# A different order of work at two places of a gated MLP: the first channel block, and the head of the first pair

## The chip, the cores and the metric

The kernel runs on one core of a Trainium2 chip. The metric is device time in microseconds (us) of one execution. The engines are TensorE (PE; its weight loads are listed apart as PEld), VectorE (DVE), ScalarE (ACT), GpSimd (POOL) and SyncE (SP, which issues the weight loads from memory).

## The reference

Two layers over 256 tokens of width 2048, in float32. Layer 0 mixes tokens by grouped-query attention, layer 1 by dilated sliding-window attention; each is followed by the gated MLP that this case is about, and a last RMS norm ends it. Cut to the MLP:

```python
D_MODEL, SEQ, D_FF, DEPTH = 2048, 256, 5632, 2

def conv_ffn(h, w_up, conv_w, conv_b, w_down):
    u = h @ w_up                                  # 256 x 2048 times 2048 x 11264
    u = depthwise_conv_width_3(u, conv_w) + conv_b   # over token positions
    gate, val = jnp.split(u, 2, axis=-1)
    return (jax.nn.silu(gate) * val) @ w_down     # 256 x 5632 times 5632 x 2048

for i in range(DEPTH):
    h = h + mixer(rms_norm(h, mix_norm[i]))
    h = h + conv_ffn(rms_norm(h, ffn_norm[i]), w_up[i], conv_w[i], conv_b[i], w_down[i])
return rms_norm(h, final_norm)
```

## The kernel before

**Products.** A float32 product is made of three passes. Every operand is split into a high part (typed F32R) and a low part, the rest; the kernel sums high x high, high x low and low x high into one accumulator. Weights arrive as raw tiles of 128 x 1024 numbers (512 KB), one load each on SP's queue, into six buffers. For each tile ACT copies the high part (`wh`, L126) and DVE subtracts it from the raw tile (`wl`, L127); there are three buffers for such pairs, four in the down projection. So every tile costs one ACT and one DVE operation, whatever is done with it.

**Up projection.** A column block is 512 of the 11264 columns. A gate block and a value block make a channel block; there are eleven, numbered 0 to 10, worked in two halves (0 to 5, 6 to 10). A column block takes four feeds, one for each quarter (0 to 3) of the 2048 inputs; a feed (`feed`) loads and splits two raw tiles and issues 24 matmuls: two tiles, two 128-row pieces each, two token halves, three passes. The accumulators are two PSUM banks. Normally `project` runs four feeds of the gate and then four of the value. Channel block 0 is special: the transposed input of the last input quarter is still being made then (`late_transpose`), so `project2` runs quarters 0, 1, 2 of the gate and of the value, then `drain` writes out what is pending, then quarter 3 of each.

**Post-processing.** When a column block is done, a generator (`up_post`) follows: ACT evacuates the two banks and DVE transposes them in 32 x 32 blocks; sixteen small copies, shared by POOL, DVE and ACT, place them in order (L430, L432, L434); ACT and DVE do the convolution; for a gate, Silu, for a value, the product with the gate and the split into high and low halves, or, in a block that the down projection treats with seven products, the seven combinations it needs (`glu_forms`). The taps of the convolution come from `taps`, called once behind gate block 0: three transposes of `cr` (L399), loaded at the start of the MLP. Generators wait in the list `pending`. `step`, called twice in a feed and once in a unit of a pair, moves the first one on by one stage; during the up projection it moves the first two.

**Down projection.** A half of the channel blocks is multiplied into `h` for two column blocks n0 and n1 at a time, a pair (`project_pair`). Its accumulators are all eight banks: C11, C21 (the two token halves for n0), C12, C22 (for n1), M1, M5, M6, M7. Its work is a list of units. A usual unit ("c", channel block, 0 to 3) takes one raw tile and 12 matmuls for two of the C banks; four of them make a channel block. A seven-product unit ("P", channel block, product) takes one tile and six matmuls; seven of them, in the order 1, 2, 5, 3, 7, 6, 4, make a channel block in the manner of Strassen and Winograd. Products 5, 7, 6 and 4 need a sum of two weight blocks first, a DVE operation of its own (L228). Product 2 adds to C11, 3 to C12, 4 to C21. Seven-product channel blocks are the first and third of a first half, and the first of a second half: 16 usual and 14 seven-product units in a first half, 16 and 7 in a second. The unit list takes one usual unit, then a seven-product and a usual one by turns, then the usual ones that are left. Before the first unit of the last channel block `drain` completes what is pending, in the first pair.

After the last seven-product unit `combine` starts (L601 to L613: the M banks are added into `h`), and after C21's last unit `first_half` adds C11 and C21 into `h` (L374, `add_residual`). C12 and C22 are added at the end. A first half has two pairs, columns (0, 1) and (2, 3), one behind the other on the same banks; a second half has one pair, and `project` for the other two column blocks.

**What sets the order.** The kernel writes its instructions in the order above, and a planner places them on the engines by its own timing: on each engine the ready instruction that was written first goes first, and the two split operations and the sums of weight blocks count as written 45 instructions earlier (`AHEAD`). An operation that is ready early can so run ahead of its place in the text; once placed, an engine's order is fixed.

Of the kernel before, what the change touches and what calls it, by code (L numbers as in the profile page):

```python
# [18 lines left out]
NPAIR = 11  # L19
# [5 lines left out]
ORDER = (1, 2, 5, 3, 7, 6, 4)  # L25
PLACE = "pava"
AHEAD = 45
NWARM = 11


@with_exitstack
def tile_encoder(ctx: ExitStack, tc: tile.TileContext, x, xT, w_a, w_ao, q_gain, k_gain, w_b, w_bo,
# [67 lines left out]
    def drain(keep=0):  # L100
        while len(pending) > keep:
            step()
# [20 lines left out]
    def split_raw(r, release=True):  # L123
        wh, wl = new_hl()
        with tc.high_priority(offset=AHEAD):
            nc.scalar.activation(wh, r, AF.Copy)  # L126
# [47 lines left out]
    def new_acc():  # L174
        bank_at[0] = (bank_at[0] + 2) % 4
        return [bank(bank_at[0] + m, "acc") for m in range(2)]

    def project(w, n, lhs, kgs, by_m=False):
        accs = new_acc()
        for i, kg in enumerate(kgs):  # L180
            end = i == len(kgs) - 1
            feed(accs, lhs, kg, w[n, kg], i == 0, end, by_m and end)
        return accs

    def project2(w, n0, n1, lhs, kgs, late, first_done, hook=None):
        a0, a1 = new_acc(), new_acc()
        early = len(kgs) - late
        for k, part in enumerate((range(early), range(early, len(kgs)))):
            if k == 1:
                drain()  # L190
            for accs, n in ((a0, n0), (a1, n1)):
                for i in part:
                    kg = kgs[i]
                    mid = hook and hook(n == n0, kg)
                    feed(accs, lhs, kg, w[n, kg], i == 0, i == len(kgs) - 1,
                         pieces=4 if hook and i < 2 else 2, mid=mid)
                if k == 1 and n == n0:
                    first_done(a0)
        return a1

    def project_pair(w, n0, n1, lhs, forms, units, late, early_done, n0_done):
        home = {1: "M1", 2: "C11", 3: "C12", 4: "C21", 5: "M5", 6: "M6", 7: "M7"}
        place = ("M1", "M5", "M6", "M7", "C11", "C21", "C12", "C22")
        b = bank_at[0]
        acc = {k: bank((4, 5, 6, 7, 2 - b, 3 - b, b, b + 1)[i], "acc") for i, k in enumerate(place)}

        def touched(u):
            return (home[u[2]],) if u[0] == "P" else (("C11", "C21"), ("C12", "C22"))[u[2] // 2]

        first, last = {}, {}  # L210
        for i, u in enumerate(units):
            for k in touched(u):
                first.setdefault(k, i)
                last[k] = i
        blocks = {}
        sums = {5: ("11", "12"), 7: ("12", "22"), 6: ("22", "11"), 4: ("21", "22")}

        def block(kg, b):
            if (kg, b) not in blocks:
                blocks[kg, b] = load_raw(w, (n0, n1)[int(b[1]) - 1], kg, int(b[0]) - 1)  # L220
            return blocks[kg, b]

        def prepare(u):
            kind, kg, p = u
            if kind == "P" and p in sums:
                dst, src = (block(kg, b) for b in sums[p])
                with tc.high_priority(offset=AHEAD):
                    nc.vector.tensor_tensor(dst, dst, src, ALU.add)  # L228
                if p == 6:
                    done_raw(blocks.pop((kg, "11")))  # L230
                elif p == 4:
                    done_raw(blocks.pop((kg, "22")))

        last_s = max(i for i, u in enumerate(units) if u[0] == "P")
        for i, (kind, kg, p) in enumerate(units):
            if i == late:
                drain()
            if kind == "c":
                r = load_raw(w, (n0, n1)[p // 2], kg, p % 2)
            else:  # L240
                b = {1: "11", 2: "21", 3: "22", 5: "11", 7: "12", 6: "22", 4: "21"}[p]
                r = block(kg, b)
            if i + 1 < len(units):
                prepare(units[i + 1])
            wh, wl = split_raw(r, kind == "c" or p in (7, 4))
            if kind == "P" and p in (7, 4):
                blocks.pop((kg, b))
            todo = []
            if kind == "c":
                for j in range(2):  # L250
                    for m, k in enumerate(touched((kind, kg, p))):
                        todo.append((k, *at(lhs[4 * kg + 2 * (p % 2) + j], m), j))
            else:
                xh, xl = forms[kg][p]
                for j in range(2):
                    todo.append((home[p], xh[:, j * P:(j + 1) * P], xl[:, j * P:(j + 1) * P], j))
            fresh = {k for k in acc if first[k] == i}
            for k, xh, xl, j in todo:
                nc.tensor.matmul(acc[k], xh, wh[:, j, :], start=k in fresh, stop=False)  # L259
                fresh.discard(k)  # L260
                nc.tensor.matmul(acc[k], xl, wh[:, j, :], start=False, stop=False)  # L261
            todo.sort(key=lambda t: (t[0], t[3]))
            for k, xh, xl, j in todo:
                nc.tensor.matmul(acc[k], xh, wl[:, j, :], start=False, stop=last[k] == i and j == 1)  # L264
            if i == last_s:
                early_done(acc)
            if i == last["C21"]:
                n0_done(acc)
            step()
        return acc  # L270
# [111 lines left out]
    def ffn(l, hT, ss_in, g_next, last, side=None):  # L382
        with tc.tile_pool(name=nm("wpool"), bufs=1) as wp, tc.tile_pool(name=nm("fpool"), bufs=1) as fp:
# [111 lines left out]
            kgs = list(range(4))  # L495
            for hf, (p0, p1) in enumerate(HALVES):
# [8 lines left out]
                for p in range(p0, p1):  # L505
                    if p - p0 in SKG[hf]:
                        fm = forms[p - p0] = {f: new_form() for f in (1, 7, 2, 5, 4, 6, 3) + (0,) * hf}
                        if hf:
                            for kt in range(4):
                                slots[4 * (p - p0) + kt] = [  # L510
                                    tuple(t[:, kt % 2 * P:(kt % 2 + 1) * P] for t in fm[f])
                                    for f in ((1, 0), (2, 4))[kt // 2]]
                    else:
                        slots.update({4 * (p - p0) + j: new_form() for j in range(4)})
                    cg, cv = ([fp.tile([P, 2, NT], F32, tag=t, name=nm(t), bufs=3) for _ in range(2)]
                              for t in ("cg", "cv"))

                    def after(hh, cg=cg, cv=cv, slots=slots, forms=forms, kg=p - p0):
                        if kg in forms:
                            return glu_forms(cg[hh], cv[hh], forms[kg], hh)  # L520
                        return glu(cg[hh], cv[hh], slots, 4 * kg + 2 * hh)

                    if p == 0:
                        def gate_done(a, cg=cg):
                            taps()
                            start(up_post(a, 0, cg))

                        va = project2(w_up[l], p, NPAIR + p, hT, kgs, 1, gate_done)
                    else:
                        start(up_post(project(w_up[l], p, hT, kgs), p, cg))  # L530
                        va = project(w_up[l], NPAIR + p, hT, kgs)
                    start(up_post(va, NPAIR + p, cv, after))
                    if p == 1 and side is not None:
                        spare.append(side(wp, fp))
# [41 lines left out]
                np_ = p1 - p0  # L576
# [7 lines left out]
                        fin.append(f)  # L584
                cs = [("c", k, i) for k in range(np_) if k not in SKG[hf] for i in range(4)]
                ps = [("P", k, p) for k in SKG[hf] for p in ORDER]
                per = max((len(cs) - 4) // len(ps), 1)
                units = [cs.pop(0)]
                for u in ps:
                    units += [u] + [cs.pop(0) for _ in range(per)]  # L590
                units += cs
                late_at = next(i for i, u in enumerate(units) if u[1] == np_ - 1)
                hl_ring.insert(0, (wp, 9))

                def hcol(m, n):
# [27 lines left out]
                    done((a["C11"], a["C21"]), n0)  # L623

                def pair(n0, n1, late):
                    acc = project_pair(wd, n0, n1, slots, forms, units, late_at if late else None,
                                       lambda a: start(combine(a, n0, n1)),
                                       lambda a: first_half(a, n0, n1))
                    done((acc["C12"], acc["C22"]), n1)
                    finished(n0, n1)  # L630
# [395 lines left out]
    hT, ss = mixer_a()  # L1026
    hT, ss = ffn(0, hT, ss, 2, False, bias_lines)
    hT, ss = mixer_b(hT, ss)
# [85 lines left out]
```

## Time and profile before

| what | value |
|---|---|
| time, median of 3 runs | 2283.02 us (2282.5 to 2283.18) |
| the profiled execution | 2283.76 us |
| its span, first to last instruction | 2281.9 us |
| around the span | 1.86 us |
| matmuls | 10169 |
| mean granted TensorE clock | 0.999 |
| up projection, channel blocks 0 to 5, layer 0 | from 269.48 us to 539.45 |
| the two pairs of its first half | to 666.25 |
| channel blocks 6 to 10 | to 883.85 |
| the pair of the second half | to 938.66 |
| the same five edges in layer 1 | 1552.69, 1818.02, 1944.68, 2162.28, 2217.60 |

Times in the rows below are microseconds from the span's start, and nanoseconds where a row gives the mean of one instruction. A row of the instructions in order of time gives start, length, engine, line, operation, tiles, shape and count; in brackets is how long the engine was idle before it, and what it waited for last. A row of grouped instructions gives the count, then busy time and the mean of one, then the idle time before them. Matmuls overlap: they are listed as about 390 ns long and start closer together than that, so a stretch's length over its matmuls tells more than their lengths.

### The profile page before, as it was taken

The page shows a single profiled execution, that of the slowest core. Times are in us where ns is not written, and L with a number is a line of the kernel's source. Part 1 is how long each engine was busy: PE and PEld are TensorE (multiplying, and loading weights), DVE is VectorE, ACT ScalarE, POOL GpSimd, SP SyncE. Part 2 cuts the span into 40 slices and gives each one's busy share as a digit, 9 for nine tenths or more (in the row PEclk, how much of TensorE's full clock was granted, in tenths as well). Part 3 has the DMA queues.
Part 4 walks back from the last instruction along what each step waited for, and adds up shares of the span by engine and source line. Part 5 has one row for each costly group of instructions (what it writes and reads, how often), then busy time and mean ns, then how long its engine had stood idle before and what let it go on. Part 6 is the DMA issues. An engine that isn't in the chain of part 4 may idle for free. (4 is left out here: it accounts for less than half of the span.)

```text
span 2281.9 us, 28779 instructions
## 1 busy us (share of the span) xinstructions
PE 2256.4 (99%) x10169; PEld 1861.7 (82%) x10169; DVE 1756.7 (77%) x2521; ACT 1392.9 (61%) x2066; POOL 198.9 (9%) x284
## 2 busy tenths in 40 slices
PE   9999999999999999999999999999999999999998
PEld 7788777888888888888888888878788888888876
DVE  6877868888877778978876876585888788687784
ACT  6565477777547777545454554454877755577763
POOL 2210002211001011010000000000101100001110
PEclk9999999999999999999999999999999999999999
DMA  8444567765666665666655555566566566566663
GB/s 298 153 148 149 186 189 217 232 190 174 221 201 189 198 190 170 218 215 204 191 175 177 177 190 166 176 186 203 178 192 194 185 212 206 189 193 189 205 212 127
DMA packets 126449, 437.42 MB, mean 192 GB/s; under 512 B 17264, under 2 KB 18032, under 8 KB 126304
## 3 DMA queue, kind: packets, MB, share of 16 engines
q1 hardware_dynamic: 119744, 425.64, 58.5%
q0 software_dynamic: 6128, 9.38, 1.6%
q8 instruction: 79, 1.29, 0.2%
q14 instruction: 66, 0.54, 0.1%
q10 hardware_dynamic: 432, 0.56, 0.1%
HBM read 429.20 MB, written 6.29 MB: 191 GB/s over the span
## 5 line engine op out<-in xcount | busy, mean ns | idle before, releaser
L127 DVE TENSOR_TENSOR wl<-raw,wh 128x1024 fp32r<-128x1024 f32 x822 | 1005.9, 1230 | 359.7 <-ACT wh L126 354.8
L126 ACT ACTIVATE wh<-raw 128x1024 fp32r<-128x1024 f32 x822 | 865.3, 1058 | 634.9 <-PE acc L153 400.1
L152 PE MATMUL acc<-wl,xh 128*128 128x512 f32 x2176 | 850.2, 391 | 6.5 <-DVE wl L127 5.9
L151 PE MATMUL acc<-wh,xh 128*128 128x512 f32 x2176 | 853.1, 392 | 0.4 <-ACT wh L162 0.4
L153 PE MATMUL acc<-wh,xh 128*128 128x512 f32 x2176 | 848.7, 390 | 0.0
L152 PEld LDWEIGHTS acc<-wl,xh 128*128 128x128 f32 x2176 | 409.0, 188 | 95.6 <-DVE wl L127 12.3
L153 PEld LDWEIGHTS acc<-wh,xh 128*128 128x128 f32 x2176 | 408.8, 188 | 84.4
L151 PEld LDWEIGHTS acc<-wh,xh 128*128 128x128 f32 x2176 | 409.2, 188 | 83.4 <-ACT wh L162 0.8
L430 POOL COPY u<-t 32x256 f32<-32x256 f32 x176 | 112.9, 642 | 1056.8 <-DVE t L421 1048.6
L259 PE MATMUL acc<-wh,ah 128*128 128x512 f32 x524 | 204.3, 390 | 0.0
L261 PE MATMUL acc<-wh,al 128*128 128x512 f32 x524 | 204.2, 390 | 0.0
L152 PE MATMUL acc<-wl,ah 128*128 128x512 f32 x480 | 188.2, 392 | 2.0 <-DVE wl L127 1.8
L151 PE MATMUL acc<-wh,ah 128*128 128x512 f32 x480 | 187.6, 391 | 0.0
L153 PE MATMUL acc<-wh,al 128*128 128x512 f32 x480 | 187.2, 390 | 0.0
L432 ACT ACTIVATE u<-t 32x256 f32<-32x256 f32 x352 | 147.7, 420 | 22.2 <-DVE t L421 14.4
L264 PE MATMUL acc<-wl,ah 128*128 128x512 f32 x524 | 147.0, 392 | 4.3 <-DVE wl L127 3.7
L264 PEld LDWEIGHTS acc<-wl,ah 128*128 128x128 f32 x524 | 97.6, 188 | 28.1 <-DVE wl L127 8.1
L259 PEld LDWEIGHTS acc<-wh,ah 128*128 128x128 f32 x524 | 98.4, 188 | 20.6
L261 PEld LDWEIGHTS acc<-wh,al 128*128 128x128 f32 x524 | 98.5, 188 | 20.5
L152 PEld LDWEIGHTS acc<-wl,ah 128*128 128x128 f32 x480 | 90.2, 188 | 23.9 <-DVE wl L127 5.8
L151 PEld LDWEIGHTS acc<-wh,ah 128*128 128x128 f32 x480 | 90.2, 188 | 18.4
L153 PEld LDWEIGHTS acc<-wh,al 128*128 128x128 f32 x480 | 90.2, 188 | 18.2
(170 smaller groups left out, 1598.9 us busy)
## 6 DMA issues: line engine op xcount, KB each, us to landing
raw<-in_w_up_dram SPq DMA_DIRECT2D x352, 512.0 KB, 4.4
raw<-in_w_down_dram SPq DMA_DIRECT2D x176, 512.0 KB, 4.6
raw<-in_w_b_dram SPq DMA_DIRECT2D x144, 512.0 KB, 4.0
raw<-in_w_bo_dram SPq DMA_DIRECT2D x48, 512.0 KB, 4.2
raw<-in_w_a_dram SPq DMA_DIRECT2D x40, 512.0 KB, 4.7
raw<-in_w_ao_dram SPq DMA_DIRECT2D x32, 512.0 KB, 4.0
raw<-in_w_a_dram SPq DMA_DIRECT2D x16, 256.0 KB, 6.8
h<-in_x_dram SPq DMA_DIRECT2D x4, 512.0 KB, 9.3
```

The lines of the kernel that those rows point to most:

```text
L126: nc.scalar.activation(wh, r, AF.Copy)
L127: nc.vector.tensor_tensor(wl, r, wh.bitcast(F32), ALU.subtract)
L151: nc.tensor.matmul(accs[m], xh, wh[:, j, :], start=st, stop=False)
L152: nc.tensor.matmul(accs[m], xh, wl[:, j, :], start=False, stop=False)
L153: nc.tensor.matmul(accs[m], xl, wh[:, j, :], start=False, stop=sp)
L259: nc.tensor.matmul(acc[k], xh, wh[:, j, :], start=k in fresh, stop=False)
L261: nc.tensor.matmul(acc[k], xl, wh[:, j, :], start=False, stop=False)
L264: nc.tensor.matmul(acc[k], xh, wl[:, j, :], start=False, stop=last[k] == i and j == 1)
L430: nc.gpsimd.tensor_copy(dst, src)
L432: nc.scalar.activation(dst, src, AF.Copy)
```

## The change

In channel block 0 of each MLP, `project_woven` takes the place of `project2`. The order of the eight feeds was gate 0, 1, 2, value 0, 1, 2, gate 3, value 3; it becomes gate 0, 1, 2, value 0, gate 3, value 1, 2, 3. The drain stands before gate 3 in both. The taps and the gate's post-processing follow gate 3 in both.

In the down projection the unit list is made for each pair. The first pair of each half (the one that drains) begins with four usual units where it had one, then alternates as before as long as usual units last. In a first half that is 4 usual, 12 times a seven-product and a usual unit, and 2 seven-product units (products 6 and 4 of the third channel block). In a second half it is 4 usual, 7 times both, and 5 usual units. The second pair of a first half keeps its list.

```diff
+WOVEN = ((0, 0), (0, 1), (0, 2), (1, 0), (0, 3), (1, 1), (1, 2), (1, 3))
+LEAD = 4
...
+    def project_woven(w, n0, n1, lhs, order, held, first_done):
+        accs = new_acc(), new_acc()
+        seen = [0, 0]
+        for i, (c, kg) in enumerate(order):
+            if i == held:
+                drain()
+            feed(accs[c], lhs, kg, w[(n0, n1)[c], kg], seen[c] == 0, seen[c] == 3)
+            seen[c] += 1
+            if c == 0 and seen[0] == 4:
+                first_done(accs[0])
+        return accs[1]
...
-                        va = project2(w_up[l], p, NPAIR + p, hT, kgs, 1, gate_done)
+                        va = project_woven(w_up[l], p, NPAIR + p, hT, WOVEN, 4, gate_done)
...
-                per = max((len(cs) - 4) // len(ps), 1)
-                units = [cs.pop(0)]
-                for u in ps:
-                    units += [u] + [cs.pop(0) for _ in range(per)]
-                units += cs
-                late_at = next(i for i, u in enumerate(units) if u[1] == np_ - 1)
+                def weave(lead):
+                    c, units = list(cs), []
+                    units += [c.pop(0) for _ in range(lead)]
+                    for u in ps:
+                        units += [u] + [c.pop(0) for _ in range(min(1, len(c)))]
+                    return units + c
...
                 def pair(n0, n1, late):
+                    units = weave(LEAD if late else 1)
+                    late_at = next(i for i, u in enumerate(units) if u[1] == np_ - 1)
```

## The prediction

> **What bounds the kernel now.** I read the page's first two parts, then what TensorE waited for, then stretches by stage, and last single instructions in order of time.
>
> ```profile
> span 2281.9 us, 28779 instructions
> ...
> PE 2256.4 (99%) x10169; PEld 1861.7 (82%) x10169; DVE 1756.7 (77%) x2521; ACT 1392.9 (61%) x2066; POOL 198.9 (9%) x284
> ```
>
> TensorE is busy for 99% of the span, so only its gaps can be won. The change adds and drops no matmul. The waits of the weight loads say where the gaps are:
>
> ```profile
> PEld acc L152 <- DVE wl L127: 18.1, 24, 1.6
> PEld acc L264 <- DVE wl L127: 8.1, 9, 1.5
> ```
>
> The columns are microseconds in total, times, longest. TensorE waits for `wl`, the low half of a weight tile, made by DVE. L152 is the usual projections, L264 the pairs of the down projection. The stretches show how much of it lies where the change works; in each, the first number is the length, and (x...) counts instructions:
>
> ```profile
> 666.25:883.85 217.60, 217.60 (x962) 180.32 (x960) 167.04 (x241) 156.06 (x238) 23.21 (x36) 1.00 0.62 194
> 298.53:315.23 16.70, 16.70 (x76) 13.80 (x75) 10.26 (x13) 9.02 (x12) 1.69 (x4) 1.00 0.62 191
> 315.23:361.63 46.40, 44.45 (x193) 35.79 (x192) 39.87 (x66) 39.85 (x66) 4.72 (x8) 1.00 0.58 176
> 1597.54:1643.93 46.39, 44.48 (x193) 35.75 (x192) 39.86 (x66) 39.84 (x66) 4.72 (x8) 1.00 0.57 173
> 603.69:666.25 62.56, 62.56 (x278) 51.83 (x276) 52.45 (x53) 31.22 (x31) 0.00 (x0) 1.00 0.61 203
> 539.45:603.69 64.24, 63.23 (x278) 51.64 (x276) 57.05 (x66) 38.83 (x50) 3.37 (x4) 1.00 0.60 196
> 1818.02:1882.12 64.10, 63.21 (x278) 51.64 (x276) 57.58 (x67) 38.78 (x50) 3.38 (x4) 1.00 0.59 197
> 883.85:938.66 54.81, 53.69 (x235) 43.79 (x234) 49.13 (x63) 33.48 (x47) 3.37 (x4) 1.00 0.62 201
> 2162.28:2217.60 55.32, 54.05 (x236) 43.62 (x234) 47.49 (x59) 33.49 (x47) 7.47 (x6) 1.00 0.61 201
> 539.45:562.71 23.26, 22.37 (x99) 18.22 (x98) 21.67 (x31) 16.43 (x28) 3.37 (x4) 1.00 0.39 118
> ```
>
> The columns after the length are TensorE, its weight loads, DVE, ACT, POOL, the granted clock, and the DMA share and rate. The first row, up-projection blocks 6 to 10 of layer 0, has no gap: 960 matmuls in 217.60 us, 0.2267 us each. One feed (24 matmuls) is then 5.44 us, a usual unit of a pair (12) 2.72, a seven-product unit (6) 1.36. A DVE split is 1.23:
>
> ```profile
> L127 DVE TENSOR_TENSOR wl<-raw,wh 128x1024 fp32r<-128x1024 f32 x822 | 1005.9, 1230 | 359.7 <-ACT wh L126 354.8
> ```
>
> What lies above 0.2267 us a matmul is the most that the change can win. Block 1 in each MLP (third and fourth row, 192 matmuls, 43.52 us): 2.88 + 2.87 = 5.75 us. First pair of first halves, against the second pair's 62.56 for the same units: 1.68 + 1.54 = 3.22. First pair of second halves, 234 matmuls or 53.04 us: 1.77 + 2.28 = 4.05. Together 13.0 us, 0.57% of the time.
>
> **Part 1, the first channel block.** Eight feeds keep their number and work; gate 3 comes as fifth instead of seventh.
>
> ```profile
> 304.17 1.06 ACT L126 ACTIVATE wh<-raw 128x1024 fp32r<-128x1024 f32 x1 [1.66 <-PE acc L153]
> ...
> 348.12 0.19 PEld L152 LDWEIGHTS acc<-wl,xh 128*128 128x128 f32 x1 [1.55 <-DVE wl L127]
> ```
>
> Before, the gate's post-processing starts at the end of gate 3, one feed ahead of the value's, and both crowd onto block 1; the last wait there is at 348.12. Ahead of that, ACT idles 1.66 us before each split. After the change the gate's part starts two feeds (10.9 us) earlier, with value 1 to 3 (16.3 us) beside it. Does it fit? Block 1 carries 39.87 us of DVE and 39.85 of ACT; at the gap-free rate of the first row, 46.40 us would carry 167.04 x 46.40 / 217.60 = 35.6 and 156.06 x 46.40 / 217.60 = 33.3. The excess, 4.3 and 6.6 us, must move. The stretch of about three feeds before block 1 has room for 16.70 - 10.26 = 6.4 us on DVE and 16.70 - 9.02 = 7.7 on ACT, so it fits, on ACT with 1.1 us to spare. Block 1 is then loaded like the gap-free blocks. The next thing late would be the value's own post-processing, now three feeds behind the gate's where later blocks have four; for that I leave 0.37 us of wait a layer. Gain: 5.75 - 0.75 = 5.0 us.
>
> What is moved earlier must find its inputs. Gate 3 needs the last four transposed tiles, and the taps need `cr`:
>
> ```profile
> 285.51 0.48 DVE L283 SCALAR_TENSOR_TENSOR xh<-ps,gain,xh 128x256 fp32r<-128x256 f32 x1 [0.54 <-ACT xh L280]
> ...
> 275.26 0.57 POOL L393 DMA_DIRECT2D cr<-in_conv_dram  x1
> ...
> DMA to landing us min/median/max: 3.9/4.8/5.2
> ...
> 1564.80 0.49 DVE L283 SCALAR_TENSOR_TENSOR xh<-ps,gain,xh 128x256 fp32r<-128x256 f32 x1 [0.54 <-ACT xh L280]
> ```
>
> Block 0 ends at 315.23 and 1597.54; four unhindered feeds before that, gate 3 would start at 293.1 and 1575.4 (less the taps' few tenths). The tiles are ready at 286.0 and 1565.3, 7 and 10 us early, so the earlier drain has nothing left to wait for. `cr` lands by about 281 (275.26 + 5.2), the taps would run near 298. Cost 0; were that cover gone, each microsecond of lateness would stop TensorE. The weight loads of value 1 and 2 go behind gate 3's on SP's queue: the same sixteen loads, each freed by the same splits, cost 0. POOL's copies of the gate move 10.9 us forward onto a queue that has nothing else there (1.69 us busy in the second row).
>
> **Part 2, four usual units ahead.**
>
> ```profile
> 540.18 1.22 DVE L228 TENSOR_TENSOR raw<-raw,raw 128x1024 f32<-128x1024 f32 x1 [3.10 <-DMA raw<-in_w_down_dram]
> ...
> 562.71 0.73 PE L264 MATMUL acc<-wl,ah 128*128 128x512 f32 x2 [0.89 <-DVE wl L127]
> ...
> 539.45:562.71 23.26, 10.81 (x10) 1.00 0.39 118
> ...
> 539.45:562.71 23.26, 3.70 (x3) 1.00 0.39 118
> ```
>
> The last two rows are the splits (L127) and the block sums of the seven-product units (L228) alone. So from the head to the worst wait DVE was busy 21.67 of 23.26 us: 10.81 of splits, 3.70 of sums, 7.16 of post-processing of the last channel block; and just before it had lost 3.10 us in front of the first sum, whose weight blocks had not landed, with splits queued behind it. In the same time the new order executes 4 + 3 x 2 = 10 units instead of 1 + 5 x 2 = 11, and needs the sums of only one or two units instead of three: DVE has 1.23 + (1.23 to 2.46) = 2.5 to 3.7 us less to do, against an excess of 1.54 to 2.28 us in a head. The first sum also moves back by three units, behind loads of single tiles. So the waits should nearly vanish; I keep 0.3 us a head. Gain: 3.22 + 4.05 - 1.2 = 6.1 us.
>
> The price is in first halves, where 16 usual units face 14 seven-product ones: with four ahead, none is left for the last two. The pair used to end product 4, usual, usual; it ends product 6, product 4. C21 takes its last matmul in product 4, and the next pair's first unit writes C21 again. Before, two units (5.44 us) covered its evacuation:
>
> ```profile
> 595.92 0.69 DVE L604 TENSOR_TENSOR cu<-acc,cu 128x512 f32<-128x512 f32 x1
> ...
> 598.25 0.39 PE L259 MATMUL acc<-wh,ah 128*128 128x512 f32 x1
> ...
> 598.25 0.68 DVE L374 TENSOR_TENSOR h<-acc,h 128x512 f32<-128x512 f32 x1
> 598.85 1.22 DVE L127 TENSOR_TENSOR wl<-raw,wh 128x1024 fp32r<-128x1024 f32 x1
> 599.98 0.69 DVE L374 TENSOR_TENSOR h<-acc,h 128x512 f32<-128x512 f32 x1
> ...
> 608.12 0.69 DVE L612 TENSOR_TENSOR cu<-acc,cu 128x512 f32<-128x512 f32 x1
> ...
> 609.85 0.70 DVE L613 TENSOR_TENSOR h<-h,cu 128x512 f32<-128x512 f32 x1
> ```
>
> Product 4 ended at 598.25; C11 and C21 were added, a split between them, by 600.67, 2.42 us later. The next unit writes C11 first and needs C21 after two matmuls (0.45 us): 1.97 us of wait if the order stays. C11 is done six units earlier in the new order, and DVE can add it ahead: 1.97 - 0.68 = 1.3. With the C21 add alone it is 0.69 + 0.16 (the last matmul's 0.39 less 0.23) - 0.45 = 0.4; with a sum and a split ahead besides, 1.97 + 1.23 = 3.2. I take 1.3, nearest to the row. The rest of the combination is behind it: M5 was released at 608.81, 10.6 us after product 4; the next pair's product 5 is due 3 x 2.72 + 2 x 1.36 = 10.9 us after it, plus the wait. That is close; 0.5 us for it, 0 to 2. Per layer 1.8, for two layers 3.6 us, between 0.8 and 10.4. Second halves keep five usual units behind the last product and pay nothing. The second pair's list of units is the old one. The drain before the last channel block comes at unit 21 instead of 24, 44.9 us into the pair; the post-processing was over at about 564, 25 us in. Cost 0. SP issues as many loads, four single tiles ahead of the first held block; the sums' own waits for loads stay.
>
> **Sum.** -5.0 - 6.1 + 3.6 = -7.5 us. The profiled execution took 2283.76 us, 0.74 above the median of 2283.02: 2276.3 against its own time, 2275.5 as a median. A difference within 0.2%, 4.6 us, is what a measurement of this kernel can hardly tell from none.
>
> **Rivals.** (B) The waits move and only half goes, 13.0 / 2 = 6.5 us, with the price of 3.6: 2280.1. In the heads, POOL's copies could do it:
>
> ```profile
> 312.65 1.88 POOL L430 COPY u<-t 32x256 f32<-32x256 f32 x4 [35.40 <-DVE t L421]
> ...
> 544.95 3.56 POOL L430 COPY u<-t 32x256 f32<-32x256 f32 x4 [21.25 <-DVE t L421]
> ```
>
> Four took 1.88 us beside DVE's copies and 3.56 beside its other work, 1.7 more. If each of the four waited for a whole split, 4 x 1.23 = 4.9, the post-processing would end 3.2 us later still and use up the 2.5 to 3.7 us won. For B speaks too that ACT's room in block 0 is only 1.1 us; against it, that the gap-free blocks hold the same copies. The Trainium skill, SBUF — State Buffer, section "SBUF: two separate sides", has such a rule: a DVE operation with two SBUF inputs and a GpSimd one hold a shared port pair for the whole instruction, and the loser fully blocks. By that rule the time is B's; the 3.56 us show a part of it, not a full split for each copy.
>
> (C) Slower: at the end of the first pair TensorE waits for the whole combination, to the end of the row at 609.85, 610.55 - 598.25 = 12.3 us a layer, because the planner puts the adds in the order written and DVE's queue delays C21 to its end. Then -11.1 + 24.6 = +13.5: 2296.5. It decides from (11.1 + 4.6) / 2 = 7.9 us a layer. Against it: banks are released one by one, and in the rows above C21's add came 1.73 us after product 4, ahead of most of the combination. The Trainium skill, TensorE: Matmul & The Clock Gate, section "HAM oscillation", says that idle gaps over about 3.4 us halve TensorE's clock for a while; by an estimate from that page each such gap would cost some 1.7 us more, 2299.9 in all. No row here shows it; the clock is 1.00 in every stretch above.
>
> (D) More: all 13.0 goes and C21 costs only 0.4 a layer: 2283.02 - 12.2 = 2270.8.
>
> **How the numbers follow.** Forecast 0.58 (2271.5 to 2278.4), B 0.23, C 0.11, D 0.08. Faster by over 0.2% are the forecast and D, 0.66; within 0.2% B, 0.23; slower C, 0.11. The range takes in the forecast, B and its spread of some 3 us, and most of D's edge: 2270.5 to 2283.5.
>
> **What would show it.** Right: block 1 near 43.5 us, its L152 waits gone, the gate's evacuation near 299; first pairs' L264 waits under 0.3 us each; and a new wait of about 1 to 2 us where the second pair of a first half begins, released by DVE L374, twice. Wrong: block 1 still over 45 us (B), a TensorE wait of over 5 us at 600 and 1880 (C), or waits at gate 3 for tiles or taps.

## The result, and the profile after

The changed kernel took 2272.17 us (median of 5 runs, 2270.06 to 2276.86) against 2283.02 us before: a ratio of 0.9954, 95% interval 0.9939 to 0.9968, or 10.85 us less. It was forecast 7.5 us less, 2275.5, range 2270.5 to 2283.5. The profiled execution took 2272.74 us, with a span of 2270.9.

Line numbers moved: the feed's matmuls are now L153 to L155, those of the pairs L273, L275 and L278, ACT's high half L128, DVE's low half L129, the sums of weight blocks L242, the adds into `h` L388. Stretches of the changed kernel (length; then busy time of TensorE, weight loads, DVE, ACT, POOL; clock, DMA share, rate). In order: blocks 6 to 10 of layer 0; the stretch ahead of channel block 1; block 1 in layer 0 and in layer 1; channel block 2 of layer 0; first and second pair of the first half, in layer 0 and then in layer 1; the pair of the second half in both layers:

```profile
663.06:880.66 217.60, 217.60 (x961) 180.25 (x960) 168.26 (x242) 156.07 (x238) 23.24 (x36) 1.00 0.61 194
298.30:315.07 16.77, 16.77 (x76) 13.85 (x75) 12.94 (x21) 15.07 (x24) 1.70 (x4) 1.00 0.53 167
315.07:358.59 43.52, 43.52 (x193) 36.04 (x192) 37.26 (x58) 33.40 (x54) 5.16 (x8) 1.00 0.61 198
1592.55:1636.07 43.52, 43.52 (x194) 36.04 (x192) 37.26 (x58) 33.38 (x54) 5.16 (x8) 1.00 0.61 198
358.59:406.77 48.18, 47.14 (x203) 37.76 (x202) 35.90 (x55) 32.25 (x51) 16.68 (x26) 1.00 0.77 229
537.81:600.37 62.56, 62.56 (x277) 51.82 (x276) 54.63 (x62) 39.40 (x50) 2.58 (x4) 1.00 0.58 188
600.37:663.06 62.69, 62.69 (x277) 51.74 (x276) 54.49 (x56) 31.76 (x31) 0.00 (x0) 1.00 0.63 213
1810.15:1872.71 62.56, 62.56 (x278) 51.80 (x276) 53.65 (x61) 38.94 (x50) 2.58 (x4) 1.00 0.57 184
1872.71:1936.20 63.49, 62.89 (x277) 51.73 (x276) 55.06 (x57) 31.73 (x31) 0.00 (x0) 1.00 0.63 215
880.66:933.70 53.04, 53.04 (x235) 43.94 (x234) 48.27 (x62) 33.70 (x47) 2.58 (x4) 1.00 0.60 205
2153.80:2206.84 53.04, 53.04 (x235) 43.92 (x234) 46.74 (x58) 33.80 (x47) 6.68 (x6) 1.00 0.61 206
```

Channel block 1 (third and fourth row) and the four first pairs now run at 0.2267 us a matmul, without a gap. The list of what the weight loads waited for begins so:

```profile
PEld acc L154 <- DVE wl L129: 12.1, 18, 1.5
...
PEld acc L273 <- DVE h L388: 1.3, 2, 1.0
```

The waits for `wl` in the pairs (8.1 us before) are gone altogether, those in the projections fell from 18.1 to 12.1. A new row is the wait for the add into `h`, where a second pair begins. The spans differ by 11.0 us, and the stretches add up to it:

| stretch | before, us | after, us | difference |
|---|---|---|---|
| channel block 1, both layers | 46.40 + 46.39 | 43.52 + 43.52 | -5.75 |
| first pairs of first halves | 64.24 + 64.10 | 62.56 + 62.56 | -3.22 |
| first pairs of second halves | 54.81 + 55.32 | 53.04 + 53.04 | -4.05 |
| second pairs of first halves | 62.56 + 62.56 | 62.69 + 63.49 | +1.06 |
| channel block 0, layer 0 | 45.76 | 44.86 | -0.90 |
| channel block 2, layer 0 | 46.77 | 48.18 | +1.41 |
| up to the first eight feeds of the attention's projection | 51.82 | 52.52 | +0.70 |
| from the last projection to the end | 64.30 | 64.05 | -0.24 |

The first three rows are all that there was to win, 13.0 us; nothing else moved by more than 0.04 us a stretch. The last two lie where the change does nothing: the first of them took 52.52 and 51.73 us in two profiles of the changed kernel, the second 63.5 to 64.3 us over the profiles of this case. The two rows of layer 0 are a matter of chance too. In block 0, DVE waits for the load of the bias table: 4.7 us before and 3.7 after, but 4.7 again in a second profile of the changed kernel, where block 0 took 45.77 us. In block 2, DVE stands before a copy whose buffer a transfer of the position bias, issued by POOL, is still reading. DVE's waits there (total, times, longest) in the kernel before, in the changed kernel, and in its variant with the gate in plain order (below):

```profile
DVE lnt L887 <- DMA scr<-lnt: 3.1, 2, 1.5
```

```profile
DVE lnt L904 <- DMA scr<-lnt: 4.7, 2, 3.3
```

```profile
DVE lnt L904 <- DMA scr<-lnt: 7.6, 2, 4.0
```

Channel block 2 took 46.77, 48.18 and 51.57 us in these three, and 46.77 where the wait was 0.2 or 0.7 us. Up to about 3 us are covered. The 51.57 us also hold a stretch at half the clock (last section).

### The profile page after: what moved, and what is told of

Its sections match the earlier page's. It is cut to its first block, busy times and chain, and to the rows that moved or that the text cites. A ratio compares the mean times of both kernels' runs of the same rounds, so it can differ in the third digit from the quotient of the medians.

```text
span 2270.9 us, 28787 instructions
## 1 busy us (share of the span) xinstructions
PE 2251.8 (99%) x10169; PEld 1861.3 (82%) x10169; DVE 1758.8 (77%) x2521; ACT 1394.8 (61%) x2066; POOL 197.2 (9%) x284
## 4 chain that ended last, share of the span: by engine, by line
PE 81%; DVE 1%; DMA 1%; issue 0%; POOL 0%; ACT 0%; POOLq 0%; DVEq 0%; ACTq 0%
PE acc L154 21%; PE acc L153 21%; PE acc L155 21%; PE acc L273 5%; PE acc L275 5%; PE acc L278 5%; DMA scr<-lnt 1%; PE ps L305 1%; DVE wl L129 1%; PE ps L1009 0%; DVE tT L334 0%; PE ps L308 0%; PE ps L309 0%; PE ps L307 0%; DVE h L388 0%
## 5 line engine op out<-in xcount | busy, mean ns | idle before, releaser
L129 DVE TENSOR_TENSOR wl<-raw,wh 128x1024 fp32r<-128x1024 f32 x822 | 1007.1, 1229 | 354.9 <-ACT wh L128 350.2
L128 ACT ACTIVATE wh<-raw 128x1024 fp32r<-128x1024 f32 x822 | 867.0, 1058 | 622.0 <-PE acc L155 394.9
L153 PE MATMUL acc<-wh,xh 128*128 128x512 f32 x2176 | 852.0, 392 | 0.8 <-ACT wh L164 0.8
L155 PE MATMUL acc<-wh,xh 128*128 128x512 f32 x2176 | 847.6, 390 | 0.0
L155 PEld LDWEIGHTS acc<-wh,xh 128*128 128x128 f32 x2176 | 408.5, 188 | 85.0
L153 PEld LDWEIGHTS acc<-wh,xh 128*128 128x128 f32 x2176 | 408.7, 188 | 84.8 <-ACT wh L164 1.6
L273 PE MATMUL acc<-wh,ah 128*128 128x512 f32 x524 | 204.1, 390 | 0.6 <-DVE h L388 0.6
L275 PE MATMUL acc<-wh,al 128*128 128x512 f32 x524 | 203.9, 389 | 0.0
L153 PE MATMUL acc<-wh,ah 128*128 128x512 f32 x480 | 187.4, 390 | 0.0
L155 PE MATMUL acc<-wh,al 128*128 128x512 f32 x480 | 187.1, 390 | 0.0
L278 PE MATMUL acc<-wl,ah 128*128 128x512 f32 x524 | 146.0, 389 | 0.0
L273 PEld LDWEIGHTS acc<-wh,ah 128*128 128x128 f32 x524 | 98.4, 188 | 21.7 <-DVE h L388 1.3
L278 PEld LDWEIGHTS acc<-wl,ah 128*128 128x128 f32 x524 | 98.4, 188 | 20.5
L275 PEld LDWEIGHTS acc<-wh,al 128*128 128x128 f32 x524 | 98.3, 188 | 20.3
L155 PEld LDWEIGHTS acc<-wh,al 128*128 128x128 f32 x480 | 90.1, 188 | 18.4
L153 PEld LDWEIGHTS acc<-wh,ah 128*128 128x128 f32 x480 | 90.2, 188 | 18.3
```

The lines of the kernel that those rows point to most:

```text
L129: nc.vector.tensor_tensor(wl, r, wh.bitcast(F32), ALU.subtract)
L153: nc.tensor.matmul(accs[m], xh, wh[:, j, :], start=st, stop=False)
L155: nc.tensor.matmul(accs[m], xl, wh[:, j, :], start=False, stop=sp)
```

## The experiments

The times of before beside the runs differ a little from one set of runs to the next (2283.55, 2284.33 and 2285.55 us), so kernels of different sets are compared by stretches and ratios. A time without a ratio is a single execution; what it shows is read from its stretches.

### Each part alone

```diff
-LEAD = 4
+LEAD = 1
```

> The new order of the first channel block alone; the unit lists are those of before. Theory (each edit works in its own place): channel block 1 falls from 46.40 and 46.39 us to 43.5 in both layers, the first pairs stay at 64.2, 64.1, 54.8 and 55.3 us, the second pairs at 62.56; time 2283.0 - 5.75 = 2277.3 us. Rival (the edits are tied, the heads of the pairs were late because DVE never caught up with block 1): the first pairs get shorter too, and the time is under 2275.

```diff
-                        va = project_woven(w_up[l], p, NPAIR + p, hT, WOVEN, 4, gate_done)
+                        va = project2(w_up[l], p, NPAIR + p, hT, kgs, 1, gate_done)
```

> Four usual units ahead alone; the first channel block is that of before. Theory: the first pairs fall to 62.56, 62.56, 53.04 and 53.04 us (7.27 us less), the second pair of each first half is up to 1 us longer; channel block 1 keeps its 46.4 us; time 2283.0 - 7.27 + 1.06 = 2276.8 us. Rival (tied edits): the first pairs keep some of their waits.

| run | time, us | ratio to before | block 1, us | first pairs, us | second pairs, us |
|---|---|---|---|---|---|
| new first block alone | 2277.82 | 0.9979 (0.997 to 0.9988) | 43.52, 43.52 | 64.37, 64.12, 54.46, 54.73 | 62.56, 62.56 |
| four ahead alone | 2278.19 | 0.9982 (0.9973 to 0.9991) | 46.47, 46.41 | 62.92, 62.56, 53.04, 53.04 | 64.05, 62.71 |

Each edit works in its own place, but for 0.36 us left in one head with four ahead alone and 1.49 us at one second pair, where at most 1 us was expected; and the parts add up: 0.21% and 0.18% against 0.46% for both, within their intervals. The rival, that the heads of the pairs were late from block 1, falls: with block 1 free of gaps the heads keep 1.4 to 1.8 us.

### The first block: how far ahead must the gate be?

```diff
-WOVEN = ((0, 0), (0, 1), (0, 2), (1, 0), (0, 3), (1, 1), (1, 2), (1, 3))
+WOVEN = ((0, 0), (0, 1), (0, 2), (1, 0), (1, 1), (0, 3), (1, 2), (1, 3))
```

The drain moves with gate 3.

> The changed kernel with gate 3 as sixth feed, behind value 1, instead of fifth. Theory (block 1 is late by the gate's post-processing that has no room before it): two feeds have two thirds of the room, 4.3 us on DVE against 4.3 needed and 5.1 on ACT against 6.6, so 0.3 to 1.5 us of waits stay in channel block 1 of each layer (43.8 to 45.0 us). Rival (it is enough that the gate's and the value's post-processing do not start one feed apart): block 1 at 43.5 us.

Windows of channel block 1 in the two layers of this run:

```profile
314.86:359.43 44.57, 44.16 (x193) 35.91 (x192) 39.21 (x63) 35.89 (x59) 5.23 (x8) 1.00 0.61 190
1592.50:1637.07 44.57, 44.15 (x194) 35.90 (x192) 39.18 (x63) 35.88 (x59) 5.22 (x8) 1.00 0.59 190
```

1.05 us of waits are left in each layer, within what the room on ACT gave, where one feed ahead had left 2.88 and three leave none. ACT still carries 35.9 us in the block, against 33.4 with three feeds. So it is the place of the gate's work that counts, and how much room stands ahead of block 1. The time was 2274.35 us.

```diff
-WOVEN = ((0, 0), (0, 1), (0, 2), (1, 0), (0, 3), (1, 1), (1, 2), (1, 3))
+WOVEN = ((0, 0), (0, 1), (0, 2), (0, 3), (1, 0), (1, 1), (1, 2), (1, 3))
```

> The changed kernel with the first channel block in the plain order, gate 0 1 2 3 and then the value. Gate 3 is due 17.3 us after the block's start in layer 0 and 16.8 in layer 1; the last transposed tile was ready 15.5 and 12.6 us after it. Theory (the tiles have cover left): block 0 and block 1 take what they take in the changed kernel (44.9 to 45.8 and 43.5 us), no TensorE wait over 0.5 us at gate 3. Rival (the cover was the two feeds of the value): gate 3 waits 1 us or more in layer 0, where DVE waits some 4 us for a small load ahead of the tiles.

Block 0 took 44.89 us and block 1 43.52; the weight loads had no wait of their own in either. On DVE, in order of time, the copy that waits for the small load and the last tile's instruction were

```profile
281.70 0.56 DVE L895 COPY lh<-rb 128x768 f32<-128x768 f32 x1 [3.75 <-DMA rb<-in_rel_bias_dram]
...
284.73 0.48 DVE L297 SCALAR_TENSOR_TENSOR xh<-ps,gain,xh 128x256 fp32r<-128x256 f32 x1 [0.55 <-ACT xh L294]
```

so the tiles were ready at 285.2, even for a gate 3 due 17.3 us after 269.6. The cover in the prediction's first part was no closer than stated. Its time of 2274.89 us has the longest wait at the bias transfers in it, and a stretch at half the clock behind that (block 2 at 51.57 us), and does not speak against the order.

### The heads of the pairs: too much work, or a blocked queue?

The prediction laid the heads to the amount of DVE's work. The rival is that the first sum of weight blocks, placed early in DVE's queue, waits about 3 us for its weights and holds the splits behind it. In the kernel before, ACT had made the high half for the next split by 538.04, but the split stands behind the sum (started at 540.18, in the prediction's rows) and came 3.28 us later:

```profile
536.98 1.06 ACT L126 ACTIVATE wh<-raw 128x1024 fp32r<-128x1024 f32 x1 [1.16 <-issue]
...
541.32 1.22 DVE L127 TENSOR_TENSOR wl<-raw,wh 128x1024 fp32r<-128x1024 f32 x1
```

```diff
-LEAD = 4
+LEAD = 2
```

> The changed kernel with two usual units ahead instead of four; the lists of first halves then end with product 6, usual, product 4, usual. Theory A (DVE has too much work at the head; each usual unit put ahead gives it 1 to 1.5 us of room against a shortfall of 1.5 to 2.3): 0.2 to 1.2 us of TensorE waits are left in each first pair, and the wait where the second pair begins is gone. Theory B (only the first sum, standing in DVE's queue in front of weights that have not landed, makes the wait): the wait goes in full if that sum comes late enough, or stays in full, 1.5 to 2.3 us, if it still waits over 2 us.

All four first pairs took the gap-free 62.56, 62.56, 53.04 and 53.04 us, and both second pairs 62.56. Two usual units do what four do, and the price at the second pair is gone, as a usual unit again stands behind product 4. The first sum stood at 537.51 in this run and waited for nothing, as the theory of the blocked queue asks; the span was 2269.2 us.

```diff
-                with tc.high_priority(offset=AHEAD):
-                    nc.vector.tensor_tensor(dst, dst, src, ALU.add)
+                nc.vector.tensor_tensor(dst, dst, src, ALU.add)
```

This is the kernel before with that edit alone.

> The kernel before, with the sums of weight blocks (L228) no longer counted as written 45 instructions earlier. Theory B (the early sum blocks DVE's queue for 3.10 us): the first sum no longer waits over 1 us with splits behind it, and the first pairs lose most of their 1.5 to 2.3 us of waits. Theory A (too much DVE work at the head): the same work is there, so 1 us or more of waits is left in each first pair; and sums made later bring waits of their own, 1.23 + 1.06 + 1.23 = 3.5 us from sum to low half.

It did not separate the two. The planner put the first sum in the same place without the priority, as DVE's instructions in order of time show:

```profile
540.95 1.23 DVE L227 TENSOR_TENSOR raw<-raw,raw 128x1024 f32<-128x1024 f32 x1 [3.13 <-DMA raw<-in_w_down_dram]
```

and the heads kept their waits, 64.58, 64.58, 54.88 and 55.31 us. What separated them was to change the products' order and nothing else, in the run with the new first block alone:

```diff
-ORDER = (1, 2, 5, 3, 7, 6, 4)
+ORDER = (1, 2, 3, 5, 7, 6, 4)
```

> The new first channel block, the old unit lists (one usual unit ahead), and the products in the order 1, 2, 3, 5, 7, 6, 4: the first sum of weight blocks comes one product and one usual unit (4.08 us) later, the work of DVE up to product 6 is the same. Theory B (the first sum waits 3.1 us for its weights at the head of DVE's queue): that wait falls under 1 us and the first pairs fall from 64.4, 64.1, 54.5 and 54.7 us to within 0.6 us of 62.56 and 53.04. Theory A (too much DVE work): the waits of 1.4 to 1.8 us a first pair stay over 1 us.

DVE's instructions in order of time show the first sum with the old order of products, then with the new one; the four rows behind them are the windows of the four first pairs with the new one:

```profile
537.61 1.23 DVE L242 TENSOR_TENSOR raw<-raw,raw 128x1024 f32<-128x1024 f32 x1 [3.27 <-DMA raw<-in_w_down_dram]
```

```profile
540.44 1.35 DVE L242 TENSOR_TENSOR raw<-raw,raw 128x1024 f32<-128x1024 f32 x1
```

```profile
535.67:598.50 62.83, 62.83 (x278) 51.76 (x276) 56.99 (x66) 39.70 (x50) 3.44 (x4) 1.00 0.62 201
1808.37:1871.20 62.83, 62.83 (x278) 51.75 (x277) 57.10 (x66) 39.59 (x50) 3.44 (x4) 1.00 0.62 201
878.66:931.92 53.26, 53.26 (x236) 43.87 (x234) 48.28 (x62) 33.82 (x47) 3.44 (x4) 1.00 0.63 207
2151.36:2204.61 53.25, 53.25 (x235) 43.87 (x234) 46.66 (x58) 33.82 (x47) 7.54 (x6) 1.00 0.65 208
```

DVE is as busy as before (57.0 us in the first pair against 57.05), no usual unit is put ahead, and 0.2 to 0.3 us a head are left of 1.4 to 1.8. The wait of the sum made the waits of TensorE. The time was 2270.26 us. The Trainium skill, TensorE: Matmul & The Clock Gate, in its section "Architectural detail: the array is 16× 32×32, not 1× 128×128", calls the queues of ACT and DVE strictly first in, first out; the traces agree, with 3.1 to 3.3 us of a ready DVE standing idle in front of one late operand.

Is it only the wait, or DVE's time as such? In the same kernel, I added work in place of the wait; the windows of its four first pairs stand behind the expectation:

```diff
-                    nc.vector.transpose(t[:, m], s[:, m])
+                    for _ in range(3 if n - NPAIR in (5, 10) else 1):
+                        nc.vector.transpose(t[:, m], s[:, m])
```

> The kernel of the run with products 1, 2, 3, 5, and one usual unit ahead, with the transposes of the last value block of each half made three times (the same result): 4 x 0.65 = 2.6 us more for DVE at the head of each first pair. Theory C (it is DVE's time that counts, lost in a wait or spent in work): of about 3.1 us lost before, 1.5 to 2.3 reached TensorE, so 1 to 2 us of waits come back in each first pair, 63.6 to 64.8 and 54.0 to 55.2 us. Theory B in its narrow form (only a split blocked behind a late load makes TensorE wait): the first pairs stay within 0.6 us of 62.83 and 53.26.

```profile
537.00:601.43 64.43, 62.97 (x277) 51.77 (x276) 60.20 (x71) 40.04 (x50) 3.30 (x4) 1.00 0.60 196
1812.95:1877.37 64.42, 62.96 (x278) 51.75 (x276) 59.79 (x71) 39.94 (x50) 3.30 (x4) 1.00 0.59 196
881.59:936.43 54.84, 53.38 (x236) 43.80 (x234) 50.49 (x66) 33.96 (x47) 3.30 (x4) 1.00 0.61 201
2157.53:2212.36 54.83, 53.37 (x236) 43.80 (x234) 48.87 (x62) 34.04 (x47) 7.41 (x6) 1.00 0.61 202
```

1.6 us came back in every head. So DVE's time counts, whether it is spent or lost; in the kernel before, it was the 3.1 us lost in front of the sum that DVE lacked.

### Against the changed kernel, and a better version

Two usual units ahead and the changed kernel, timed on one chip:

> Two usual units ahead, timed. From the traces it should lose the 1.06 us that the changed kernel pays at the start of the second pairs and nothing else: 1 us under the changed kernel on the same chip, 2270 to 2272 us. If the waits at small loads in layer 0 (up to 3.3 us, by chance) decide, the two can't be told apart.

> The changed kernel once more, beside two usual units ahead: 2271 to 2273 us; the same stretches as in its first profile, but for channel block 2 of layer 0, which I expect to change with the wait of DVE for a small load through memory (46.8 us where that wait is under 2 us, up to 48.2 where it is 3.3).

Two ahead took 2271.30 us (0.9940, 0.9926 to 0.9953), four ahead 2275.39 us (0.9957, 0.9945 to 0.9970), against 2284.33. The changed kernel had been expected at 2271 to 2273 us and came out above. The intervals overlap; the time doesn't tell them apart. The stretches do in one point: the second pairs took 62.56 and 62.56 us with two, 63.49 and 62.95 with four. Channel block 2 of layer 0 took 48.44 and 48.22 us.

The last version puts the pieces together: the new first block, two usual units ahead, the products in the order 1, 2, 3, 5, 7, 6, 4, and the bias transfers further apart.

```diff
-LEAD = 4
+LEAD = 2
-ORDER = (1, 2, 5, 3, 7, 6, 4)
+ORDER = (1, 2, 3, 5, 7, 6, 4)
...
-                for _ in range(2):
+                for _ in range(4):
                     yield
                 c0, w = ((0, 512), (512, 256), (768, 256))[b // 2]
```

> The new first channel block, two usual units ahead, products in the order 1, 2, 3, 5, 7, 6, 4, and the six steps of the position bias in layer 0 spread over twice as many steps (four empty ones ahead of each in place of two). All pairs at 62.56 and 53.04 us; DVE no longer waits over 1 us for the small loads of channel block 2, whose length of 46.8 to 48.4 us is spread over more blocks; 2283 to 2284 less 13 to 14.5 us, 2268.5 to 2271 us, the best version. If those small loads cost nothing on the whole, it is the time of two usual units ahead, 2271.3 us.

It took 2269.73 us (2269.07 to 2270.05), 0.9932 of before (0.9918 to 0.9947): the fastest median, and the narrowest spread of the versions with five runs or more. Its pairs are all free of gaps. DVE no longer waits for the bias transfers; channel blocks 2 and 3 of layer 0 together took 45.81 + 44.96 = 90.77 us, which is what they took before in a lucky run (46.77 + 44.00). Its interval touches the changed kernel's, so a lead over it of 1 to 2 us is likely by the stretches but not shown by the time.

## Why the prediction was right or wrong

**The sum.** The time fell by 10.85 us where 7.5 were forecast. All three terms came out better than stated, the first block by 0.75 us, the heads by 1.17 and the price by 2.54; stretches that the sum left out, by chance, added 0.97. So 12.0 us belong to the change, and by that luck the time came nearer to the forecast than the terms did.

**What can be won.** Right. The excess over 0.2267 us a matmul was 13.0 us, and all of it went.

**The first block.** Right in its mechanism; the gain was 5.75 us, not 5.0. The 0.75 kept back for a late value did not come. In the stretch ahead of block 1, ACT went from 9.02 of 16.70 us to 15.07 of 16.77: 6.1 us moved, near the 6.6 reckoned, into a room of 7.7. The run with gate 3 one feed later shows that the room sets the waits. The reckoning of the fit was kinder than it should have been: it scaled the gap-free rate to 46.40 us, but a block without gaps lasts 43.52, which carries 33.4 us of DVE and 31.2 of ACT at that rate, so 8.6 us of ACT would have had to move, more than the room of 7.7. Block 1 was not loaded like the gap-free blocks either: it carried 37.26 us of DVE and 33.40 of ACT, and still had no gap. The excess did not have to go in full. Tiles and taps were in time, as stated, and even in plain order.

**The heads.** The size was nearly right (7.27 us instead of 6.1), the reason mostly not. The step that failed is "DVE has 2.5 to 3.7 us less to do". The runs put the other half of that paragraph in its place: the 3.10 us lost in front of the first sum, which I had named and not counted. In the first 23.26 us of the changed kernel's first pair DVE was busy for 22.32 us, with 11.05 of splits and 3.67 of sums, three of them as before, against 21.67, 10.81 and 3.70: it did no less work, and stood idle less.

```profile
537.81:561.07 23.26, 23.26 (x104) 19.29 (x103) 22.32 (x32) 18.10 (x29) 2.58 (x4) 1.00 0.40 133
...
537.81:561.07 23.26, 11.05 (x9) 1.00 0.40 133
...
537.81:561.07 23.26, 3.67 (x3) 1.00 0.40 133
```

With the wait alone taken away, 0.2 to 0.3 us were left in a head; with two units ahead, nothing. The four units worked because the first sum stands later in the queue than its weights; in the changed kernel's DVE, in order of time, it has no idle time before it:

```profile
543.71 1.23 DVE L242 TENSOR_TENSOR raw<-raw,raw 128x1024 f32<-128x1024 f32 x1
```

**The price at the second pair.** It is there, in its place and released by the add named, but 1.06 us (0.13 + 0.93) instead of 3.6. TensorE and then DVE around it in layer 1, in order of time:

```profile
1872.71 0.39 PE L273 MATMUL acc<-wh,ah 128*128 128x512 f32 x1
...
1874.83 0.50 PE L273 MATMUL acc<-wh,ah 128*128 128x512 f32 x1 [0.60 <-DVE h L388]
```

```profile
1872.36 0.68 DVE L388 TENSOR_TENSOR h<-acc,h 128x512 f32<-128x512 f32 x1
1872.96 1.22 DVE L129 TENSOR_TENSOR wl<-raw,wh 128x1024 fp32r<-128x1024 f32 x1
1874.09 0.68 DVE L388 TENSOR_TENSOR h<-acc,h 128x512 f32<-128x512 f32 x1
```

The C21 add ends 2.06 us after product 4, with a split ahead of it, not far from the 2.42 before. But the planner had regrouped the next unit: the six matmuls for C11 first (1872.71), then the six for C21 (1874.83). So C21 was due 1.36 us after product 4 and not 0.45, and the wait was 0.76 us. My step "needs C21 after two matmuls" was wrong by that. The 0.5 us for M5 never showed. The cost goes with how late DVE comes to the C21 add: over five profiles with four units ahead that add ended 1.30 to 2.69 us after product 4, always with a split between it and the C11 add, and cost 0.1 to 1.5 us a layer.

**What was not in the sum.** The bias table and the bias transfers, -0.90 and +1.41 us, and +0.46 at both ends of the program.

**The rivals.** The waits did not move (B). POOL's copies, on which it rested, took 2.76 us for four in the head of the changed kernel, against 3.56 before. POOL's four in one row, then the second of them alone, then the DVE split beside it:

```profile
539.50 2.76 POOL L444 COPY u<-t 32x256 f32<-32x256 f32 x4 [17.44 <-DVE t L435]
...
540.08 1.28 POOL L444 COPY u<-t 32x256 f32<-32x256 f32 x1
...
539.79 1.31 DVE L129 TENSOR_TENSOR wl<-raw,wh 128x1024 fp32r<-128x1024 f32 x1
```

The Trainium skill, SBUF — State Buffer, "SBUF: two separate sides", has the loser of the shared port block for a whole instruction. The trace agrees for the single copy: it took 1.28 us where the three others took 0.39 to 0.51, and ended 0.26 us after the split. What failed in B is the count. A split ahead of each copy would have made 1.88 + 4 x 1.23 = 6.8 us; but one split fell beside the four copies in the changed kernel, and a split and a sum before, which cost 0.9 and 1.7 us.

C did not come: no wait in the pairs exceeded 1.0 us, and the clock stayed at 1.00 in these stretches. That a gap can halve the clock did show, in another run and place (last section). D, with 12.2 us, lies closest to what the stretches of the change show, 12.0; I had given it too small a chance, because I kept back residues for which no row spoke.

## What to carry to other kernels

Before reckoning an engine's work, list where it stood idle at the head of its queue in front of one late operand: a single wait of 3 us can make what looks like overload some 20 us later, and moving one instruction behind its data is cheaper than reordering everything. Where the post-processing of two blocks crowds, start the first one earlier, in a stretch whose engines have idle time; how much idle time there is tells how much earlier. Leave a unit of other work behind the last writer of an accumulator that is needed again at once.

## What the runs showed of the hardware that was not expected

Transfers of 128 and 256 KB issued by POOL for the position bias landed between 4.1 and 17.8 us after issue in the changed kernel's profile, and DVE's wait on them was 0.2 to 7.6 us in total over twelve profiles of nearly the same program. The line is from the view of that buffer's instructions in the changed kernel:

```profile
DMA to landing us min/median/max: 4.1/8.6/17.8
```

With an in-order DVE behind them this moved channel block 2 between 46.77 and 48.44 us, and to 51.57 us together with something else: in the run with the gate in plain order, TensorE stood still for 2.55 us behind one such wait, and the granted clock was then 0.50 for 3.41 us, with matmuls 0.43 us apart. That alone costs about 1.7 us, half of 3.41. TensorE in order of time, then the stretch:

```profile
402.18 0.50 PE L154 MATMUL acc<-wl,xh 128*128 128x512 f32 x1 [2.55 <-DVE wl L129]
...
403.03 0.63 PE L154 MATMUL acc<-wl,xh 128*128 128x512 f32 x1
403.46 0.63 PE L155 MATMUL acc<-wh,xh 128*128 128x512 f32 x1
...
402.90:406.31 3.41, 3.41 (x10) 2.65 (x9) 2.15 (x2) 2.18 (x3) 0.73 (x2) 0.50 0.74 192
```

The profile of the run with two usual units ahead (2271.03 us) has the same near its start: a gap of 2.16 us, then 3.41 us at 0.50. The gaps of up to 1.46 us in the other profiles were not followed by it. So a DVE wait of 4 us can cost TensorE more than the gap it leaves.

Both may be why five runs of the changed kernel spread over 6.8 us: the longest, 2276.86 us, is the only one whose mean granted clock was 0.998 and not 0.999, as in the two profiles with a stretch at half the clock. That link was not tested further than in the last version, whose five runs lie within 1 us, all at 0.999.
